# A decoder layer on one core: the rotary table's chain moved next to the opening, and the first tokens loaded from ScalarE's queue

## The chip, the cores and the metric

The kernel runs on one core of a Trainium2 chip. The core has five engines that work side by side and wait for each other through semaphores: TensorE (PE in the profile; PEld is its loading of weights), VectorE (DVE), ScalarE (ACT), GpSimd (POOL) and SyncE (SP). Here SyncE only issues transfers (SPq in the profile). Matrix products go to PSUM, everything else lives in SBUF, and 16 DMA engines bring weights and tokens from HBM.

The metric is device time in microseconds for one execution, as the median of several runs. The profile is taken from one further execution; its span runs from the first to the last instruction of the core.

## The reference: what is computed

One layer of a decoder with 256 positions (batch 1), model width 1024, all in float32:

```python
xn = rmsnorm(h, norm_mix_g)
q_a, k_a, v_a, q_b, f_b, i_b, og_b, g_a, g_b = split_cols(xn @ w_in)   # nine widths of 1024
y_a = moba_attention(q_a, k_a, v_a, positions) @ w_br_attn             # rotary on q_a and k_a
y_b = hgrn2(q_b, f_b, i_b, og_b, lb, hgrn_norm_g) @ w_br_hgrn
h = h + (sigmoid(g_a) * y_a + sigmoid(g_b) * y_b) @ w_out
h = h + memory_cross_attention(rmsnorm(h, norm_x_g), rmsnorm(mem, norm_mem_g), wq_x, wkv_x, wo_x)
gu = rmsnorm(h, norm_ffn_g) @ w_ffn_in
h = h + (silu(gu[:, :2816]) * gu[:, 2816:]) @ w_ffn_out
out = rmsnorm(h, final_norm_g)
```

The rotary embedding turns pairs of features of q_a and k_a by an angle, position times inverse frequency. Its sine and cosine are needed once per layer, as two small tables of 256 positions by 32 frequencies. With 256 positions the attention has a single block, so it is plain causal attention.

## The kernel before, in words

**Weights.** All weight matrices are cut on the host into 97 units of 128 x 2048 floats (1 MB), in the order in which TensorE consumes them (`plan`, `lay`). A unit T covers 512 columns and 512 rows, which TensorE takes in four steps of 128 rows for each of two halves of the tokens. Float32 accuracy is made from three products: each operand is split into a rounded high half and the low half that is left, and high x high, high x low and low x high are added up in PSUM (`mm3`, `mm3t`).

**Preparing a unit** is `prep`: a transfer brings the unit into one of two buffers `raw`; ScalarE rounds it to `hi`; the subtraction `lo = raw - hi` (L185) gives the low half. A unit is handled in two pieces of 1024 columns. Of each piece VectorE subtracts 576 columns and GpSimd 448, except for the units listed in `ALONE` (0 to 7), of which VectorE does all. There are three buffers for `hi` and three for `lo`. `nxt` keeps two units prepared ahead of the one in use, so a unit's raw buffer comes free, and the transfer of the unit two later may start, when its subtraction is done.

**The opening.** Units 0 and 1 (the forget gate's columns, upper half of the rows) are loaded in four pieces of 512 columns each, so that TensorE can start early; unit 1 has a buffer of its own. The tokens, transposed, arrive in five pieces: eight groups of 128 features, cut 1, 1, 2, 2, 2. `part_x` multiplies a group by the norm's gain and splits it into Xh and Xl. All these transfers, the small vector `gv` first, are issued by SyncE one after the other, tokens and weights alternating. After them come units 2 and 3, the constants `cst` (with the identity matrix, a mask, and in its last 32 columns the inverse frequencies), `posi` (the positions), unit 4, the tokens H in rows (1 MB), and the masks `lm`; a transfer waits for the completion of the one eight places before it whose semaphore it takes over. TensorE first runs 18 multiplications of zeros (`warm`), then the gate's product from units 0 and 1, then from 2 and 3.

**The norm's factor.** The products are made with the tokens as they are; the factor 1/rms is applied when a result leaves PSUM. ScalarE squares the two halves of H and adds them up (`junk`, `ssqx`), VectorE makes the mean (L274), GpSimd takes it to the power -0.5 (L276): that is `r_x`. VectorE halves it (`r_half`, L444). Four instructions on ScalarE (`fth`, L391) then take the gate's product out of PSUM with that factor, TensorE turns the result (L369), and ScalarE and VectorE write it to fT.

**The rotary chain.** `rope_tables` runs on GpSimd: it multiplies frequencies by positions, reduces the angle to one turn in several steps of added precision, and folds it, 47 small instructions on 128 x 64 elements, each of which needs the one before. Two sines on ScalarE follow, and eight multiplications by `r_x` on GpSimd give the tables Ct and St. It is a generator: `start(rt)` puts it among the background work, of which `tick` takes a step after every unit. Ct and St are used by `ev_rope`, well after q_b, i_b and v_a.

**The order of work.** TensorE's instructions run in the order in which they are written (`manual_schedule`). For the other engines a scheduler in the tile framework chooses the order, except that a few instructions are pinned with `keep_in_program_order`. In the kernel before, it puts GpSimd's work like this: the positions to float, the first of two angle products, r_x, the rest of the chain (45 instructions), then the twelve products `Tt` of the recurrence (L554), then GpSimd's share of unit 8's subtraction, which is the first that it has. Unit 8 is the first one of i_b; TensorE takes it after the second half of q_b.

Of the kernel before, what the change touches and what calls it, by code (L numbers as in the profile page):

```python
# [18 lines left out]
S, D, NK = 256, 1024, 8  # L19
# [18 lines left out]
C_W = 544  # L38
# [31 lines left out]
def lay(ws):  # L70
    out = np.empty((len(ORDER), 128, 2048), np.float32)
    for i, u in enumerate(ORDER):
        if u[0] == "F":
            w = ws[u[1]][:, u[2]:u[2] + 256]
            out[i].reshape(128, 8, 256)[...] = w.reshape(8, 128, 256).transpose(1, 0, 2)
        elif u[0] == "T":
            w = ws[u[1]][u[3] * 512:(u[3] + 1) * 512, u[2]:u[2] + 512]
            out[i].reshape(128, 4, 512)[...] = w.reshape(4, 128, 512).transpose(1, 0, 2)
# [33 lines left out]
def build(tc, A, out):  # L112
    nc = tc.nc
    V, SC, G, PE, SY = nc.vector, nc.scalar, nc.gpsimd, nc.tensor, nc.sync
    with ExitStack() as ctx:
# [26 lines left out]
        cst = cp.tile([128, C_W], F32, name="cst")  # L142
# [12 lines left out]


        ready = {}
# [2 lines left out]
        def prep(tags=None, raw=None):  # L160
            i = made[0]
            made[0] += 1
            first = i < 2
            if raw is None:
                raw = wr.tile([128, 2048], F32, name="raw", tag="raw")
            if tags is None:
                hi = wh.tile([128, 2048], F32R, name="hi", tag="hi")
                lo = wl.tile([128, 2048], F32R, name="lo", tag="lo")
            else:
                hi = big(tags[0], "hix", (128, 2048), F32R)  # L170
                lo = big(tags[1], "lox", (128, 2048), F32R)
            pieces = 4 if first else 2
            n = 2048 // pieces
            if not first:
                SY.dma_start(raw, A["w"][i])
            for c in range(pieces):
                a = slice(c * n, (c + 1) * n)
                if first:
                    SY.dma_start(raw[:, a], A["w"][i][:, a])
                    yield  # L180
                SC.activation(hi[:, a], raw[:, a], AF.Copy)  # L181
                cut = (c + 1) * n - (0 if i in ALONE else POOL_COLS // pieces)
                for eng, b in ((V, slice(c * n, cut)), (G, slice(cut, (c + 1) * n))):
                    if b.start < b.stop:
                        eng.tensor_tensor(lo[:, b], raw[:, b], hi[:, b].bitcast(F32), op=ALU.subtract)  # L185
            ready[i] = (hi, lo)
# [129 lines left out]
        def part_x(k):  # L316
            g1 = gv[:, V_MIX + k:V_MIX + k + 1]
            SC.activation(Xh[:, k], xraw[:, k], AF.Copy, scale=g1)
            V.scalar_tensor_tensor(Xl[:, k], xraw[:, k], g1, Xh[:, k].bitcast(F32),
                                   op0=ALU.mult, op1=ALU.subtract)  # L320

        def take_x(a, b):
            SY.dma_start(xraw[:, a:b], A["xT"][:, a:b])

        for k in range(4):
            if k in (0, 1, 2):
                take_x(k, (1, 2, 4)[k])
            next(opening[0])
            part_x(k)
        run(opening[0])  # L330
        run(opening[1])
        for k in (4, 6):
            take_x(k, k + 2)
        for k in range(4, 8):
            part_x(k)

        lbt = cp.tile([128, 8], F32, name="lbt")
        oml = cp.tile([128, 8], F32, name="oml")
# [101 lines left out]
        for t in range(2):  # L440
            SC.activation(junk[:, t], H[:, t], AF.Square, accum_out=ssqx[:, t:t + 1])
        r_x = rstd_of(ssqx, "x")
        r_half = cp.tile([128, 2], F32, name="r_half")
        V.tensor_scalar(r_half, r_x, 0.5, None, op0=ALU.mult)  # L444
        ev = ev_f(0)
# [6 lines left out]
            t_part(pss[1][t], w, X, t, 1)  # L452
            ev(t, pss[1][t])
        tick()


        Ct = cp.tile([128, 2, 64], F32, name="Ct")
        St = cp.tile([128, 2, 64], F32, name="St")

        def rope_tables():  # L460
            posf = small("posf", [2])
            G.tensor_copy(posf, posi)
            q = cp.tile([128, 7, 2, 32], F32, name="rt")
            ang, m, mh, ml, r, t, u = (q[:, i] for i in range(7))
            for i in range(2):
                G.tensor_scalar(ang[:, i], cst[:, C_IF:C_IF + 32], posf[:, i:i + 1], None, op0=ALU.mult)

            def rnd(o, src, c):
                G.tensor_scalar(o, src, c, None, op0=ALU.mult)
                G.tensor_scalar(o, o, RND, None, op0=ALU.add)  # L470
                G.tensor_scalar(o, o, RND, None, op0=ALU.subtract)

            def acc(o, a, c, b):
                G.tensor_scalar(u, a, float(c), None, op0=ALU.mult)
                G.tensor_tensor(o, u, b, op=ALU.add)

            rnd(m, ang, 1.0 / (TWO_PI * 1024.0))
            rnd(mh, m, 1.0 / 1024.0)
            G.tensor_scalar(mh, mh, 1024.0, None, op0=ALU.mult)
            G.tensor_tensor(ml, m, mh, op=ALU.subtract)  # L480
            yield 1
            acc(r, mh, -D1, ang)
            acc(r, ml, -D1, r)
            acc(r, mh, -D2, r)
            acc(t, ml, -D2, r)
            acc(t, mh, -D3, t)
            rnd(t, t, 1.0 / TWO_PI)
            yield 1
            for a, c in ((t, C1), (ml, D2), (mh, D3), (t, C2), (ml, D3), (t, C3), (m, D4)):
                acc(r, a, -c, r)  # L490
            lim = 3.1415925
            G.tensor_scalar(t, r, lim, -TWO_PI, op0=ALU.is_gt, op1=ALU.mult)
            G.tensor_scalar(ml, r, -lim, TWO_PI, op0=ALU.is_lt, op1=ALU.mult)
            G.tensor_tensor(r, r, t, op=ALU.add)
            G.tensor_tensor(r, r, ml, op=ALU.add)
            yield 1
            G.tensor_scalar(r, r, lim, -lim, op0=ALU.min, op1=ALU.max)
            G.tensor_scalar(t, r, 0.0, -2.0, op0=ALU.is_gt, op1=ALU.mult)
            G.tensor_scalar(t, t, 1.0, None, op0=ALU.add)
            G.tensor_tensor(t, t, r, op=ALU.mult)  # L500
            G.tensor_scalar(t, t, TWO_PI / 4, None, op0=ALU.add)
            for _ in range(4):
                yield 1
            tc.keep_in_program_order(SC.activation(m, r, AF.Sin))
            tc.keep_in_program_order(SC.activation(mh, t, AF.Sin))
            for i in range(2):
                rs = r_x[:, i:i + 1]
                for c in range(2):
                    G.tensor_scalar(Ct[:, i, c * 32:(c + 1) * 32], mh[:, i], rs, None, op0=ALU.mult)
                G.tensor_scalar(St[:, i, 0:32], m[:, i], rs, -1.0, op0=ALU.mult, op1=ALU.mult)  # L510
                G.tensor_scalar(St[:, i, 32:64], m[:, i], rs, None, op0=ALU.mult)

        rt = rope_tables()

        AT = big("B9", "AT", (128, 24, 128))
        at3 = AT[:, 0:16]
# [648 lines left out]
```

## Time and profile before

| | |
|---|---|
| median of 3 runs | 638.72 us (638.44 to 639.66) |
| the profiled execution's own time | 639.19 us |
| its span | 637.4 us |
| mean granted clock of TensorE | 0.991 |
| bytes moved | 107.5 MB, 169 GB/s over the span |
| TensorE busy | 619.7 us, 97% of the span |

The profiled execution took 0.47 us longer than the median, and 1.8 us longer than its own span. In the lines below a group of instructions is named by line, engine, operation and tiles (`out<-in`); times in a timeline are start and duration in microseconds from the span's start, with the idle time before and what ended it in brackets. A row of waits gives who waited for whom, then total, number and longest. Busy time of TensorE is no measure of its efficiency; what can be read is where it stands idle, at which clock it runs, and how far apart its matmuls start.

### The profile page before, as it was taken

The numbers are of one execution on the slowest core, as the hardware profiler recorded it, in microseconds if no ns is written. First come the engines' busy times: TensorE is split into PE (matmuls) and PEld (weight loads), VectorE is DVE, ScalarE is ACT, GpSimd is POOL, SyncE is SP. The second block draws the span as 40 slices with busy tenths as digits, with TensorE's granted clock in tenths as the row PEclk, the third lists the DMA queues.
The fourth block names the chain that finished last, engine by engine and source line by source line (L and its number), as shares of the span: only waits on it lengthen the run. The fifth ranks groups of instructions, "written<-read, shape, count | busy, mean of one in ns | idle before, by whom it ended". The sixth has DMA issues, their size and how long they took to land.

```text
span 637.4 us, 8670 instructions
## 1 busy us (share of the span) xinstructions
PE 619.7 (97%) x3262; PEld 521.4 (82%) x3262; DVE 380.0 (60%) x649; ACT 326.2 (51%) x513; POOL 367.1 (58%) x289
## 2 busy tenths in 40 slices
PE   7996999999999999999999999999999999999995
PEld 6784888888887777778889999888888888888884
DVE  6462677888857777685646446664444444444433
ACT  6683544433457667673455444554444444444433
POOL 0588555455644564446857767656566555666552
PEclk9998999999999999999999999999999999999998
DMA  8760633443533333535544454462355544455511
GB/s 270 297 240 20 249 147 133 164 171 137 190 132 134 133 132 133 198 135 197 196 159 173 174 192 165 173 250 77 132 193 199 192 176 174 189 194 198 198 66 66
DMA packets 17177, 107.52 MB, mean 169 GB/s; under 512 B 2160, under 2 KB 2544, under 8 KB 4720
## 3 DMA queue, kind: packets, MB, share of 16 engines
q1 hardware_dynamic: 17136, 106.98, 46.6%
q8 instruction: 25, 0.41, 0.3%
q14 instruction: 16, 0.13, 0.1%
HBM read 105.92 MB, written 1.05 MB: 168 GB/s over the span
## 4 chain that ended last, share of the span: by engine, by line
PE 89%; POOL 5%; DMA 3%; issue 1%; SPq 1%; ACT 0%; DVE 0%; POOLq 0%; DVEq 0%; ACTq 0%
PE pst L225 13%; PE pst L226 13%; PE pst L227 13%; PE psi L225 6%; PE psi L227 6%; PE psi L226 6%; PE acc L227 3%; PE acc L226 3%; PE acc L225 3%; PE psf L220 2%; PE psf L221 2%; PE psf L222 2%; PE lp L582 2%; DMA H<-xtok 2%; PE pso L225 1%; PE pso L227 1%
## 5 line engine op out<-in xcount | busy, mean ns | idle before, releaser
L185 POOL TENSOR_TENSOR lo<-raw,hi 128x448 fp32r<-128x448 f32 x174 | 271.0, 1572 | 190.0 <-ACT hi L181 183.3
L181 ACT ACTIVATE hi<-raw 128x1024 fp32r<-128x1024 f32 (+1 forms) x194 | 196.3, 1037 | 199.7 <-PE pst L227 62.7
L185 DVE TENSOR_TENSOR lo<-raw,hi 128x576 fp32r<-128x576 f32 (+2 forms) x194 | 194.1, 1005 | 143.5 <-ACT hi L181 126.7
L226 PE MATMUL pst<-lo,Xh 128*128 128x512 f32 x256 | 100.7, 393 | 6.1 <-POOL lo L185 6.1
L225 PE MATMUL pst<-hi,Xh 128*128 128x512 f32 x256 | 103.8, 405 | 0.0
L227 PE MATMUL pst<-hi,Xl 128*128 128x512 f32 x256 | 100.6, 393 | 0.0
L225 PE MATMUL psi<-hi,h2h 128*128 128x512 f32 x176 | 69.6, 396 | 0.0
L227 PE MATMUL psi<-hi,h2l 128*128 128x512 f32 x176 | 68.7, 390 | 0.0
L226 PE MATMUL psi<-lo,h2h 128*128 128x512 f32 x176 | 68.6, 390 | 0.0
L226 PEld LDWEIGHTS pst<-lo,Xh 128*128 128x128 f32 x256 | 48.7, 190 | 15.7 <-POOL lo L185 6.5
L227 PEld LDWEIGHTS pst<-hi,Xl 128*128 128x128 f32 x256 | 48.5, 189 | 10.3
L225 PEld LDWEIGHTS pst<-hi,Xh 128*128 128x128 f32 x256 | 48.6, 190 | 10.1 <-issue 0.7
L227 PEld LDWEIGHTS psi<-hi,h2l 128*128 128x128 f32 x176 | 33.1, 188 | 7.1
L226 PEld LDWEIGHTS psi<-lo,h2h 128*128 128x128 f32 x176 | 33.1, 188 | 6.5
L225 PEld LDWEIGHTS psi<-hi,h2h 128*128 128x128 f32 x176 | 33.1, 188 | 6.5
L225 PE MATMUL acc<-hi,hid 128*128 128x512 f32 x88 | 34.3, 390 | 0.0
L226 PE MATMUL acc<-lo,hid 128*128 128x512 f32 x88 | 34.3, 389 | 0.0
L227 PE MATMUL acc<-hi,hid 128*128 128x512 f32 x88 | 34.3, 389 | 0.0
L1056 DVE SCALAR_TENSOR_TENSOR fu<-psi,r_h,fg 128x256 f32<-128x256 f32 x22 | 10.6, 483 | 26.1 <-ACT fg L1054 26.1
L1054 ACT ACTIVATE fg<-psi,r_h 128x256 f32<-128x256 f32 x22 | 10.5, 475 | 29.9 <-PE psi L227 29.9
L227 PEld LDWEIGHTS acc<-hi,hid 128*128 128x128 f32 x88 | 16.5, 188 | 3.4
L225 PEld LDWEIGHTS acc<-hi,hid 128*128 128x128 f32 x88 | 16.5, 188 | 3.4
(338 smaller groups left out, 1172.1 us busy)
## 6 DMA issues: line engine op xcount, KB each, us to landing
raw<-w SPq DMA_DIRECT2D x95, 1024.0 KB, 4.8
raw<-w SPq DMA_DIRECT2D x8, 256.0 KB, 5.8
H<-xtok SPq DMA_DIRECT2D x1, 1024.0 KB, 10.2
mraw<-mT SPq DMA_DIRECT2D x1, 1024.0 KB, 7.0
out<-H SPq DMA_DIRECT2D x4, 256.0 KB, 2.2
xraw<-xT SPq DMA_DIRECT2D x3, 256.0 KB, 5.9
gfin<-gfin SPq DMA_DIRECT2D x1, 512.0 KB, 4.9
cst<-cst SPq DMA_DIRECT2D x1, 272.0 KB, 8.9
```

The lines of the kernel that those rows point to most:

```text
L181: SC.activation(hi[:, a], raw[:, a], AF.Copy)
L185: eng.tensor_tensor(lo[:, b], raw[:, b], hi[:, b].bitcast(F32), op=ALU.subtract)
L220: PE.matmul(ps, lh, rh, start=first, stop=False)
L221: PE.matmul(ps, lh, rl, start=False, stop=False)
L222: PE.matmul(ps, ll, rh, start=False, stop=last)
L225: PE.matmul(ps, xh, h, start=first, stop=False)
L226: PE.matmul(ps, xh, l, start=False, stop=False)
L227: PE.matmul(ps, xl, h, start=False, stop=last)
L582: PE.matmul(ps[:, j], KS[:, a0 + j], QQ[:, a0 + j], start=True, stop=True)
L1054: SC.activation(g, ps[:, 0:256], AF.Silu, scale=r)
L1056: V.scalar_tensor_tensor(u, ps[:, 256:512], r, g, op0=ALU.mult, op1=ALU.mult)
```

## The change

Six things are done together.

1. `rope_tables` stands right behind the opening's last token work. Its first half (24 instructions, to the end of its second part) is issued there, its second half (parts three and four) right behind r_x. The sines and the tables Ct and St are issued where they were, by `tick`.
2. From there to the end of q_b's products GpSimd is under `manual_schedule`: its instructions run in the order in which they are written. The first half of the chain so stands ahead of r_x, the second half between r_x and Tt. Ct and St come between the subtractions of unit 9 and unit 10.
3. The inverse frequencies get an array and a tile of their own, `ifq` (128 x 32). It and the positions are issued by SyncE right behind the last token piece, ahead of units 2 and 3; the positions stood behind units 2 and 3 and `cst` before.
4. `gv` and the first three token pieces are issued by ScalarE. Its function table's load, which stood first, comes behind the first two of these transfers. SyncE starts with the four pieces of unit 0.
5. On the host, each of the eight pieces of units 0 and 1, and each of the five token pieces, is laid out as one contiguous block.
6. `ALONE` is 0 to 8: VectorE subtracts all of unit 8 as well.

With the new positions the scheduler also changes some of the others' order: on ScalarE the first `fth` stands ahead of the two `hi` instructions of unit 4 and the other three behind them, where all four stood behind; the two first `hi` pieces of unit 0 stand ahead of the second token group; the exponentials of `lbt` come behind the opening. TensorE's order is the same, instruction for instruction.

```diff
-ALONE = range(8)
+ALONE = range(9)
+TOKENS = ((0, 1), (1, 2), (2, 4), (4, 6), (6, 8))
...
+            if i < 2:
+                out[i].reshape(4, 128, 512)[...] = w.reshape(4, 128, 512)
+            else:
+                out[i].reshape(128, 4, 512)[...] = w.reshape(4, 128, 512).transpose(1, 0, 2)
...
+        def piece(ap, a):
+            flat = ap.rearrange("p c -> (p c)")
+            return flat[128 * a.start:128 * a.stop].rearrange("(p c) -> p c", p=128)
...
+        ifq = cp.tile([128, 32], F32, name="ifq")
...
-        SY.dma_start(gv, A["gv"])
+        SC.dma_start(gv, A["gv"])
...
-        warm_act = cp.tile([128, 1], F32, name="warm_act")
-        SC.activation(warm_act, ones, AF.Exp)
...
-                    SY.dma_start(raw[:, a], A["w"][i][:, a])
+                    SY.dma_start(raw[:, a], piece(A["w"][i], a))
...
-        def take_x(a, b):
-            SY.dma_start(xraw[:, a:b], A["xT"][:, a:b])
-
+        def take_x(eng, a, b):
+            eng.dma_start(xraw[:, a:b].rearrange("p k c -> p (k c)"), piece(A["xT"], slice(256 * a, 256 * b)))
+
+        take_x(SC, *TOKENS[0])
+        warm_act = cp.tile([128, 1], F32, name="warm_act")
+        SC.activation(warm_act, ones, AF.Exp)
+        for piece_x in TOKENS[1:3]:
+            take_x(SC, *piece_x)
         for k in range(4):
-            if k in (0, 1, 2):
-                take_x(k, (1, 2, 4)[k])
             next(opening[0])
             part_x(k)
         run(opening[0])
         run(opening[1])
-        for k in (4, 6):
-            take_x(k, k + 2)
+        for piece_x in TOKENS[3:]:
+            take_x(SY, *piece_x)
+        SY.dma_start(ifq, A["ifq"])
+        SY.dma_start(posi, A["pos"])
         for k in range(4, 8):
             part_x(k)
...
+        rt = rope_tables()
+        region = tc.manual_schedule(engines={mybir.EngineType.Pool})
+        region.__enter__()
+        next(rt)
+        next(rt)
...
         SY.dma_start(cst, A["cst"])
-        SY.dma_start(posi, A["pos"])
...
         r_x = rstd_of(ssqx, "x")
+        next(rt)
+        next(rt)
...
         start(rt)
         for c in range(2):
             gemm_t(X, ev_q(c))
+        region.__exit__(None, None, None)
```

More of the change, by code (lines that the diff above doesn't have):

```diff
@@ L77, in lay @@
             w = ws[u[1]][u[3] * 512:(u[3] + 1) * 512, u[2]:u[2] + 512]
-            out[i].reshape(128, 4, 512)[...] = w.reshape(4, 128, 512).transpose(1, 0, 2)
+            if i < 2:
+                out[i].reshape(4, 128, 512)[...] = w.reshape(4, 128, 512)
+            else:
+                out[i].reshape(128, 4, 512)[...] = w.reshape(4, 128, 512).transpose(1, 0, 2)
         elif u[0] == "I":
@@ L137, in small @@
             return sp.tile([128] + list(shape), F32, name=name)
+        def piece(ap, a):
+            flat = ap.rearrange("p c -> (p c)")
+            return flat[128 * a.start:128 * a.stop].rearrange("(p c) -> p c", p=128)
         def bank(name, shape=(128, 512)):
             return sm.tile(list(shape), F32, name=name, tag="sm")
-        cst = cp.tile([128, C_W], F32, name="cst")
+        cst = cp.tile([128, C_IF], F32, name="cst")
         gv = cp.tile([128, 56], F32, name="gv")
@@ L331, in build, with rope_tables, rnd, acc @@
         run(opening[1])
-        for k in (4, 6):
-            take_x(k, k + 2)
+        for piece_x in TOKENS[3:]:
+            take_x(SY, *piece_x)
+        SY.dma_start(ifq, A["ifq"])
+        SY.dma_start(posi, A["pos"])
         for k in range(4, 8):
             part_x(k)
+        Ct = cp.tile([128, 2, 64], F32, name="Ct")
+        St = cp.tile([128, 2, 64], F32, name="St")
+        def rope_tables():
+            posf = small("posf", [2])
+            G.tensor_copy(posf, posi)
+            q = cp.tile([128, 7, 2, 32], F32, name="rt")
+            ang, m, mh, ml, r, t, u = (q[:, i] for i in range(7))
+            for i in range(2):
+                G.tensor_scalar(ang[:, i], ifq, posf[:, i:i + 1], None, op0=ALU.mult)
+            def rnd(o, src, c):
+                G.tensor_scalar(o, src, c, None, op0=ALU.mult)
+                G.tensor_scalar(o, o, RND, None, op0=ALU.add)
+                G.tensor_scalar(o, o, RND, None, op0=ALU.subtract)
+            def acc(o, a, c, b):
+                G.tensor_scalar(u, a, float(c), None, op0=ALU.mult)
+                G.tensor_tensor(o, u, b, op=ALU.add)
+            rnd(m, ang, 1.0 / (TWO_PI * 1024.0))
+            rnd(mh, m, 1.0 / 1024.0)
+            G.tensor_scalar(mh, mh, 1024.0, None, op0=ALU.mult)
+            G.tensor_tensor(ml, m, mh, op=ALU.subtract)
+            yield 1
+            acc(r, mh, -D1, ang)
+            acc(r, ml, -D1, r)
+            acc(r, mh, -D2, r)
+            acc(t, ml, -D2, r)
+            acc(t, mh, -D3, t)
+            rnd(t, t, 1.0 / TWO_PI)
+            yield 1
+            for a, c in ((t, C1), (ml, D2), (mh, D3), (t, C2), (ml, D3), (t, C3), (m, D4)):
+                acc(r, a, -c, r)
+            lim = 3.1415925
+            G.tensor_scalar(t, r, lim, -TWO_PI, op0=ALU.is_gt, op1=ALU.mult)
+            G.tensor_scalar(ml, r, -lim, TWO_PI, op0=ALU.is_lt, op1=ALU.mult)
+            G.tensor_tensor(r, r, t, op=ALU.add)
+            G.tensor_tensor(r, r, ml, op=ALU.add)
+            yield 1
+            G.tensor_scalar(r, r, lim, -lim, op0=ALU.min, op1=ALU.max)
+            G.tensor_scalar(t, r, 0.0, -2.0, op0=ALU.is_gt, op1=ALU.mult)
+            G.tensor_scalar(t, t, 1.0, None, op0=ALU.add)
+            G.tensor_tensor(t, t, r, op=ALU.mult)
+            G.tensor_scalar(t, t, TWO_PI / 4, None, op0=ALU.add)
+            for _ in range(4):
+                yield 1
+            tc.keep_in_program_order(SC.activation(m, r, AF.Sin))
+            tc.keep_in_program_order(SC.activation(mh, t, AF.Sin))
+            for i in range(2):
+                rs = r_x[:, i:i + 1]
+                for c in range(2):
+                    G.tensor_scalar(Ct[:, i, c * 32:(c + 1) * 32], mh[:, i], rs, None, op0=ALU.mult)
+                G.tensor_scalar(St[:, i, 0:32], m[:, i], rs, -1.0, op0=ALU.mult, op1=ALU.mult)
+                G.tensor_scalar(St[:, i, 32:64], m[:, i], rs, None, op0=ALU.mult)
@@ L454, in build @@
         tick()
[L457 to L511, printed above, removed]
@@ L1137, in feats, with by_piece @@
         return np.ascontiguousarray(v[0].T.reshape(8, 128, S).transpose(1, 0, 2))
+    def by_piece(v):
+        return np.concatenate([v[:, i:j].reshape(-1) for i, j in TOKENS]).reshape(128, 8 * S)
     ws = {k: a[k][0] for k in ("w_in", "w_br_attn", "w_br_hgrn", "w_out", "wq_x", "wkv_x", "wo_x",
@@ L1144 @@
         "w": lay(ws),
-        "xT": feats(a["x"]),
+        "xT": by_piece(feats(a["x"])),
         "xtok": tokens(a["x"]),
         "mT": feats(a["mem"]),
+        "ifq": np.ascontiguousarray(cst[:, C_IF:]),
         "pos": np.ascontiguousarray(a["positions"][0].reshape(2, 128).T),
@@ L1152 @@
         "gfin": np.ascontiguousarray(a["final_norm_g"].reshape(1, D)),
-        "cst": cst,
+        "cst": np.ascontiguousarray(cst[:, :C_IF]),
         "lm": lm,
```

1 line of the change is left out of this document (removed).

## The prediction

> **What bounds the kernel now.** I read the page's first part, then who TensorE (PE) waits for, then the chain of waits, then windows round the one long wait, then the engines' timelines of the opening.
>
> ```profile
> PE 619.7 (97%) x3262; PEld 521.4 (82%) x3262; DVE 380.0 (60%) x649; ACT 326.2 (51%) x513; POOL 367.1 (58%) x289
> ```
> ```profile
> PE pst L226 <- POOL lo L185: 6.1, 1, 6.1
> PE psg L429 <- ACT hi L181: 2.0, 2, 1.2
> ...
> PE psg L226 <- DVE lo L185: 0.7, 1, 0.7
> ```
>
> PE is busy 97% and, once started, waits for another engine only in these places: 2.7 us in the opening, and once 6.1 us for the low half of a weight unit that GpSimd (POOL) makes. Everything after that wait runs at PE's own pace, so whatever PE gains or loses up to there should reach the end one for one. The chain of waits tells why POOL was late:
>
> ```profile
> 23.23 2.20 ACT junk L441 x4
> ...
> 25.71 0.73 POOL r_x L276
> 26.44 0.37 POOL rt L466
> ...
> 54.43 0.37 POOL rt L501
> 54.80 1.01 POOL Tt L554
> ...
> 61.07 1.14 POOL lo L185
> 62.25 0.80 PE pst L226
> 63.05 0.43 PE pst L227
> ...
> 619.88 0.23 PE acc L227
> ```
>
> From 26.44 to 54.80 POOL works off the rotary chain, then the products Tt, and only at 61.07 the weight unit. The windows (busy time and instructions of PE, PEld, DVE, ACT, POOL, then granted clock, DMA share, GB/s) show a second price of that wait:
>
> ```profile
> 55.00:56.20 1.20, 1.16 (x6) 0.62 (x4) 0.00 (x0) 0.69 (x1) 1.12 (x2) 1.00 0.02 7
> 56.20:59.20 3.00, 0.00 (x0) 0.00 (x0) 0.00 (x0) 0.00 (x0) 2.61 (x7) 1.00 0.00 0
> 59.20:62.20 3.00, 0.00 (x0) 0.00 (x0) 0.00 (x0) 0.00 (x0) 2.69 (x7) 0.51 0.00 0
> 62.20:66.20 4.00, 3.95 (x10) 3.15 (x11) 0.00 (x0) 0.00 (x0) 3.29 (x3) 0.51 0.42 125
> 66.20:70.00 3.80, 3.80 (x23) 3.29 (x22) 0.65 (x1) 1.74 (x2) 0.60 (x1) 1.00 1.00 407
> ```
>
> About 3 us into the idle time the clock falls to half, and it stays there until about 66.1. About nine matmuls run in that stretch at 0.43 us instead of 0.23: 9 x 0.20 = 1.8 us. The wait is worth 6.1 + 1.8 = 7.9 us.
>
> **The change part by part.** The sum is made against the profiled execution's own 639.19 us (span 637.4); the median of the three runs is 638.72, so I subtract from the median.
>
> *The rotary chain moves forward: -7.9.* Its second half now stands right behind r_x and its first half ahead of it. The rows I price it with:
>
> ```profile
> 20.86 0.18 POOL L462 CAST posf<-posi 128x2 f32<-128x2 int32 x1 [20.44 <-DMA posi<-pos]
> 21.15 2.51 POOL L466 TENSOR_SCALAR rt<-cst,posf 128x32 f32<-128x32 f32 x1
> 27.35 0.38 POOL L470 TENSOR_SCALAR rt<-rt 128x64 f32<-128x64 f32 x1
> 28.27 1.41 POOL L469 TENSOR_SCALAR rt<-rt 128x64 f32<-128x64 f32 x1
> 29.76 1.09 POOL L470 TENSOR_SCALAR rt<-rt 128x64 f32<-128x64 f32 x1
> 31.85 0.33 POOL L480 TENSOR_TENSOR rt<-rt 128x64 f32<-128x64 f32 x1
> 35.33 0.32 POOL L475 TENSOR_TENSOR rt<-rt 128x64 f32<-128x64 f32 x1
> 40.89 0.37 POOL L471 TENSOR_SCALAR rt<-rt 128x64 f32<-128x64 f32 x1
> ```
> ```profile
> 14.37 1.81 DVE L319 SCALAR_TENSOR_TENSOR Xl<-xraw,gv,Xh 128x256 fp32r<-128x256 f32 x4 [0.43 <-ACT Xh L318]
> 21.14 2.36 DVE L185 TENSOR_TENSOR lo<-raw,hi 128x1024 fp32r<-128x1024 f32 x2 [0.23 <-ACT hi L181]
> 26.48 0.17 DVE L444 TENSOR_SCALAR r_half<-r_x 128x2 f32<-128x2 f32 x1 [0.85 <-POOL r_x L276]
> 28.22 2.40 DVE L185 TENSOR_TENSOR lo<-raw,hi 128x1024 fp32r<-128x1024 f32 x2 [1.57 <-ACT hi L181]
> 34.94 0.53 DVE L384 TENSOR_SCALAR fT<-fT__353,gate_a,gate_b 128x256 f32<-128x256 f32 x1
> ```
>
> A quiet POOL step takes 0.37 us (scalar form) or 0.33 (two tensors), each with 0.08 to the next. Beside a VectorE subtraction lo<-raw,hi it takes 1.41, 1.09 or 2.51 instead; beside fT, which reads PSUM, it keeps 0.32. From 26.44 to 41.26 (end of the step at 40.89) run 16 scalar and 6 two-tensor steps: 14.8 us, of which 16 x 0.45 + 6 x 0.40 = 9.6 are work and 5.2 are stretch from six subtractions of 1.2 us, 0.87 each.
>
> After the change, 24 steps stand ahead of r_x: 0.3 + 17 x 0.45 + 6 x 0.40 = 10.3 us quiet. r_x itself, the second half (23 steps, about 10 us and three pairs of subtractions, 15 us), the twelve Tt (6.3 us, 54.80 to 61.07) then end near 51, and PE wants that weight unit at 56 or later. Besides, unit 8 is now split by VectorE alone (one more in ALONE), and POOL's next one, unit 9, is wanted a unit later still. So the 6.1 us go, and the half clock with them. VectorE's extra share (1024 columns of a piece at 1.2 us instead of 576, so 2 x 1.2 x 448/1024) is 1.0 us and due by PE's 56; in the stretch in which its queue comes to it VectorE is busy less than half the time,
>
> ```profile
> 45.00:50.00 5.00, 5.00 (x28) 4.25 (x27) 2.11 (x3) 3.17 (x4) 4.23 (x10) 1.00 0.56 213
> ```
>
> so nothing; if that cover went, it would cost the 1.0 us. The eight Ct/St steps move ahead of unit 10; that unit is wanted two units (over 11 us) after the Sin that releases them: nothing.
>
> *The price: r_x now waits for the first half.* It starts when positions land. They are moved from behind two whole weight units and cst to right behind the last token piece:
>
> ```profile
> 13.82 1.84 ACT L318 ACTIVATE Xh<-xraw,gv 128x256 fp32r<-128x256 f32 x4 [0.61 <-DMA xraw<-xT]
> 17.45 2.01 ACT L181 ACTIVATE hi<-raw 128x1024 fp32r<-128x1024 f32 x2 [1.79 <-DMA raw<-w]
> 29.04 2.50 ACT L391 ACTIVATE fth<-psg,r_half 128x512 f32<-128x512 f32 x4
> ```
>
> The last token piece was there by the third Xh, 14.7. With the gain of the opening (0.7, below) positions land near 14.0. Then 10.3 quiet, plus the subtractions of units 2 and 3 (four, 0.87 each: 3.5), plus the four Xl of 0.45, never seen beside POOL: between nothing (like fT) and 4 x 0.45 x 0.73 = 1.3 (like lo); they too read two SBUF tensors, but some are over by then, so 0.7. Sum 28.5 for the start of r_x, against 25.71; the sum of squares will be ready before 25.45. Bounds 26.5 and 30.5.
>
> Who is queued behind it: r_half and then unit 4's subtraction on VectorE; on ScalarE, where the order now puts one fth ahead of unit 4's two hi and three behind them, all of these. From r_x's start: 0.73, then 0.2 for r_half, fth 0.65, two hi 2.0, second fth 0.65: 4.3 us. PE's transposes need both:
>
> ```profile
> 30.66 0.60 PE L369 MATMUL fT__353<-cst,fth 128*128 128x128 f32 x4
> ```
>
> They started at 30.66 with PE busy up to them; now 28.5 + 4.3 = 32.8. PE is 2.1 us behind there, after an idle time of 2.1 + 0.7 = 2.8 us. That delay is kept to the end: +2.1 (bounds 0.1 and 4.1, from 26.5 and 30.5).
>
> *Tokens on ScalarE's queue, contiguous first pieces: 0.7 earlier in the opening, then used up.*
>
> ```profile
> 1.16 0.42 SPq L323 DMA_DIRECT2D xraw<-xT  x1
> 1.63 0.42 SPq L179 DMA_DIRECT2D raw<-w  x1
> ```
> ```profile
> 1.50:5.40 3.90, 3.78 (x18) 3.57 (x18) 1.85 (x11) 1.42 (x4) 0.00 (x0) 1.00 0.69 170
> 8.50:18.80 10.30, 10.24 (x45) 8.29 (x45) 7.42 (x14) 7.70 (x15) 0.00 (x0) 1.00 1.02 384
> ```
>
> The first weight piece is issued at 0.7 instead of 1.63. From 8.5 on the transfers are the limit (share 1.02, 384 GB/s), so all that counts is what moves before: 170 GB/s for 3.9 us, where 384 would save 2.2 us. Whether address order helps there the trace cannot tell; bounds -0.5 (two queues in each other's way) and 1.9. I take 0.7, nearer to the 0.9 of the earlier issue. ScalarE pays four issues of 0.42 with its table load between them, before it has data; SyncE's queue loses these four and gains the one for ifq (16 KB): nothing for both, as long as the transfers are the limit. The opening's 0.7 is worth something at the end only if r_x isn't late; here PE just waits 0.7 longer at the transposes.
>
> Sum: 638.72 - 7.9 + 2.1 = **632.9 us**.
>
> [...] In the rows a subtraction of 1.2 us holds POOL 0.87 us. [...] The clock fell 3 us into the idle time above, and mine is 2.8. [...]
>
> **The rivals.**
> - *The first half is done in time* (0.18). Positions land at 12.5, or VectorE's work falls before or after. The earliest r_x is the sum of squares, about 25; then 25 + 4.3 is before 30.66 - 0.7 and PE keeps the opening's gain too: 638.72 - 7.9 - 0.7 = 630.1, down to 629.4. Against it: 10.3 quiet us from 14.0 already end at 24.3, and units 2 and 3 are split inside that time.
> - *POOL is held longer and PE's clock falls* (0.16). The row at 21.15 is stretched by 2.14 us beside 2.36 of subtraction, 0.91 of it. On 4.7 + 1.8 us that gives 5.9 and r_x at 30.2; PE is 3.8 late and idle for 4.5, more than the 3 us of the windows, so another 1.8 goes: 638.72 - 7.9 + 5.6 = 636.4.
> - *A new wait replaces the old one* (0.08), at unit 9 or 10: POOL still does Tt, Ct/St and two units there. A third of the old wait back: 635.
> - *Slower* (0.08): r_x so late that it eats the gain. From 7.9 - 1.8 = 6.1 us late on PE, an r_x at 30.66 + 6.1 - 4.3 = 32.5, it decides. That needs positions at 18 instead of 14, as if they still queued behind a weight unit (they landed at 20.86 before): at 19.5, r_x at 34.0 gives 7.6 + 1.8 - 7.9, 640.2.
> - *Nothing* (0.05): 638.7, if gain and price cancel.
>
> **How the numbers follow.** The forecast's own case has 0.45, with 631 to 635 for r_x between 26.6 and 30.6; the others as given, which adds to 1. A measurement of this kernel can tell about 0.2% (1.3 us) from no change. Faster by more: 0.45 + 0.18 + 0.16 + 0.08 = 0.87, same 0.05, slower 0.08. The range leaves out the last two cases: from 629.4 to 636.8.
>
> **What would show it.** Right: no wait of PE for POOL's lo near 56 and full clock there; positions landing near 14 and POOL's chain starting with them; r_x near 28.5, behind POOL's own step and not behind the sum of squares; a new wait of PE of 2 to 3 us at the transposes fT, for ScalarE's fth; Tt over by about 51. Wrong: r_x still at 25 to 26 (then more is gained), a half clock near 33, or a wait at units 8 to 10 in the old one's place.

## The result, and the profile after

The changed kernel takes 632.63 us (median of 5 executions, 631.75 to 634.07). On the same chip the kernel before took 638.44 us (638.3 to 639.66). The ratio is 0.9899, with a 95% interval of 0.9887 to 0.9912: 6.4 us less. The profiled execution of the changed kernel is the longest of its five: 634.07 us, span 632.3.

The page's first part for the changed kernel, then its table of who TensorE waits for (total us, times, longest):

```profile
PE 620.0 (98%) x3262; PEld 521.5 (82%) x3262; DVE 384.8 (61%) x649; ACT 325.1 (51%) x513; POOL 366.7 (58%) x287
```
```profile
PE fT__408 L445 <- ACT fth L467: 2.3, 2, 2.1
...
PE psg L504 <- ACT hi L189: 0.7, 1, 0.7
PE psg L504 <- ACT Xh L326: 0.3, 1, 0.3
```

TensorE has the same work, 620 us in 3262 instructions. The wait of 6.1 us for GpSimd's lo is gone. In its place stands a new one of 2.3 us at the transposes fT, for ScalarE's fth.

How far the gain has come, and whether any of it is given back, is read at one late landmark in the two chains of waits: TensorE's transposes h1T, and the last piece of the end. Kernel before, then changed kernel (start, us, what):

```profile
345.05 0.87 PE h1T L904 x8
...
630.88 1.79 issue
```
```profile
340.00 0.87 PE h1T L923 x8
...
625.82 1.79 issue
```

From h1T to the end both take 285.8 us. The changed kernel is 5.05 us ahead at h1T and 5.06 at the end, so in these two executions all of the difference arises before, and nothing of it is lost later.

The first stage, engine by engine (start, us, engine, line, operation; in brackets how long the engine had been idle, which is no point in time, and what ended it). GpSimd of the changed kernel:

```profile
12.94 0.96 POOL L356 CAST posf<-posi 128x2 f32<-128x2 int32 x1 [12.52 <-DMA posi<-pos]
14.01 1.60 POOL L360 TENSOR_SCALAR rt<-ifq,posf 128x32 f32<-128x32 f32 x2
...
17.52 1.16 POOL L364 TENSOR_SCALAR rt<-rt 128x64 f32<-128x64 f32 x1
18.76 1.09 POOL L365 TENSOR_SCALAR rt<-rt 128x64 f32<-128x64 f32 x1
19.93 1.32 POOL L373 TENSOR_SCALAR rt<-rt 128x64 f32<-128x64 f32 x1
21.33 1.04 POOL L374 TENSOR_TENSOR rt<-rt 128x64 f32<-128x64 f32 x1
...
27.99 0.73 POOL L284 TENSOR_TENSOR r_x<-v__339,nhalf 128x2 f32<-128x2 f32 x1
...
44.68 1.03 POOL L572 TENSOR_TENSOR Tt<-fT 128x512 f32<-128x512 f32 x1
...
53.57 1.16 POOL L193 TENSOR_TENSOR lo<-raw,hi 128x448 fp32r<-128x448 f32 x1
```

VectorE, ScalarE and TensorE of the changed kernel in the same stretch:

```profile
11.37 2.49 DVE L193 TENSOR_TENSOR lo<-raw,hi 128x512 fp32r<-128x512 f32 x4
13.78 1.66 DVE L327 SCALAR_TENSOR_TENSOR Xl<-xraw,gv,Xh 128x256 fp32r<-128x256 f32 x4
...
17.22 2.40 DVE L193 TENSOR_TENSOR lo<-raw,hi 128x1024 fp32r<-128x1024 f32 x2 [0.61 <-ACT hi L189]
19.79 2.40 DVE L193 TENSOR_TENSOR lo<-raw,hi 128x1024 fp32r<-128x1024 f32 x2 [0.18 <-ACT hi L189]
24.04 0.17 DVE L282 TENSOR_SCALAR v__339<-ssqx 128x2 f32<-128x2 f32 x1 [1.85 <-ACT junk L516]
28.75 0.17 DVE L521 TENSOR_SCALAR r_half<-r_x 128x2 f32<-128x2 f32 x1 [4.54 <-POOL r_x L284]
```
```profile
29.02 0.69 ACT L467 ACTIVATE fth<-psg,r_half 128x512 f32<-128x512 f32 x1 [5.01 <-DVE r_half L521]
29.60 1.99 ACT L189 ACTIVATE hi<-raw 128x1024 fp32r<-128x1024 f32 x2
31.50 1.83 ACT L467 ACTIVATE fth<-psg,r_half 128x512 f32<-128x512 f32 x3
```
```profile
29.19 0.39 PE L235 MATMUL psg<-hi,Xl 128*128 128x512 f32 x1
29.76 0.33 PE L445 MATMUL fT__408<-cst,fth 128*128 128x128 f32 x1 [0.18 <-ACT fth L467]
32.23 0.55 PE L445 MATMUL fT__408<-cst,fth 128*128 128x128 f32 x3 [2.14 <-ACT fth L467]
```

What to see: GpSimd's first step starts at 12.94, when the positions are there. The sum of squares' scaled value v stands at 24.04 + 0.17 = 24.2, but r_x starts at 27.99, right behind GpSimd's own chain. ScalarE is idle for 5.01 us until r_half, and then does one fth, the two hi of unit 4 and only then the second fth. TensorE is through with its matmuls at 29.6 and gets the second fth at 32.2.

Windows of the changed kernel (TensorE, its weight loads, VectorE, ScalarE, GpSimd: busy us and instructions; then granted clock, DMA share, GB/s):

```profile
30.00:32.00 2.00, 0.09 (x1) 0.00 (x0) 1.32 (x2) 2.00 (x3) 1.75 (x4) 1.00 0.00 0
32.00:33.70 1.70, 1.47 (x10) 1.39 (x11) 1.17 (x1) 1.70 (x5) 1.53 (x3) 0.99 0.00 0
33.70:37.10 3.40, 3.40 (x9) 2.66 (x8) 2.88 (x3) 2.95 (x5) 2.97 (x6) 0.50 0.71 272
...
55.00:60.00 5.00, 5.00 (x24) 4.14 (x23) 1.71 (x3) 3.09 (x7) 2.19 (x3) 1.00 0.52 185
```

At 55 to 60, where the 6.1 us stood, TensorE is busy throughout at full clock. But from 33.7 to 37.1, after it has been working again for 1.5 us, its clock is half: at 0.43 us a matmul instead of 0.23 these 3.4 us cost about 1.6.

### The profile page after: what moved, and what is told of

It is laid out like the page before. It is cut to its first block, busy times and chain, and to the rows that moved or that the text cites. A ratio compares the mean times of both kernels' runs of the same rounds, so it can differ in the third digit from the quotient of the medians.

```text
span 632.3 us, 8666 instructions
## 1 busy us (share of the span) xinstructions
PE 620.0 (98%) x3262; PEld 521.5 (82%) x3262; DVE 384.8 (61%) x649; ACT 325.1 (51%) x513; POOL 366.7 (58%) x287
## 4 chain that ended last, share of the span: by engine, by line
PE 94%; issue 3%; POOL 2%; ACT 1%; DVE 0%; POOLq 0%; ACTq 0%
PE pst L233 14%; PE pst L235 14%; PE pst L234 14%; PE psi L233 6%; PE psi L235 6%; PE psi L234 6%; PE acc L235 3%; PE acc L234 3%; PE acc L233 3%; PE psf L229 2%; PE psf L228 2%; PE psf L230 2%; PE lp L600 2%; PE pso L233 1%; PE pso L235 1%
## 5 line engine op out<-in xcount | busy, mean ns | idle before, releaser
L193 DVE TENSOR_TENSOR lo<-raw,hi 128x576 fp32r<-128x576 f32 (+2 forms) x194 | 198.1, 1028 | 126.5 <-ACT hi L189 125.3
L233 PE MATMUL psi<-hi,h2h 128*128 128x512 f32 x176 | 69.6, 395 | 0.0
L235 PEld LDWEIGHTS acc<-hi,hid 128*128 128x128 f32 x88 | 16.5, 188 | 3.4
L234 PEld LDWEIGHTS acc<-lo,hid 128*128 128x128 f32 x88 | 16.5, 188 | 3.4
```

The costliest lines, as they stand in the source:

```text
L233: PE.matmul(ps, xh, h, start=first, stop=False)
L234: PE.matmul(ps, xh, l, start=False, stop=False)
L235: PE.matmul(ps, xl, h, start=False, stop=last)
```

## The experiments

None of the eleven kernels leaves out any of the reference's work. The gain in the last column is (1 - ratio) times 638.7 us, so that the runs of different chips stand on one scale; "wait" is TensorE's longest one behind the opening.

| kernel | median us (range) | ratio to before [95%] | wait | gain us |
|---|---|---|---|---|
| the change | 632.63 (631.75-634.07) | 0.9899 [0.9887, 0.9912] | fth 2.3 | 6.4 |
| before + unit 8 alone | 637.08 (636.51-637.31) | 0.9966 [0.9953, 0.9978] | QQ 3.9 | 2.2 |
| change without unit 8 alone | 633.05 (631.38-634.5) | 0.9902 [0.9885, 0.992] | fth 2.1 | 6.3 |
| change with the old opening | 633.82 (633.07-635.31) | 0.992 [0.9906, 0.9935] | fth 1.8 | 5.1 |
| before + the opening | 637.32 (636.23-638.73) | 0.9969 [0.996, 0.9979] | lo 5.6 | 2.0 |
| before + opening + unit 8 | 634.92 (633.65-635.76) | 0.9933 [0.9919, 0.9947] | QQ 3.6 | 4.3 |
| change, r_x earlier | 630.24 (629.08-631.26) | 0.9863 [0.9846, 0.988] | QQ 0.4 | 8.8 |
| change, hi ahead of fth | 630.24 (630.02-631.19) | 0.9869 [0.9852, 0.9885] | fth 0.6 | 8.4 |
| both of these | 629.43 (628.85-630.67) | 0.9854 [0.9838, 0.9869] | none | 9.3 |
| change, filler in the wait | 633.26 (632.3-633.85) | 0.991 [0.9895, 0.9924] | fth 1.2 | 5.7 |
| change, r_x later | 642.01 (641.01-642.79) | 1.0042 [1.0029, 1.0056] | fth 9.8 | -2.7 |

### Unit 8 split by VectorE alone, in the kernel before

```diff
-ALONE = range(8)
+ALONE = range(9)
```

> The kernel before with one edit: unit 8 is subtracted by VectorE alone; chain, r_x and transfers stay. Theory A (what counts is which unit first needs GpSimd after the chain): before, the chain and Tt end at 61.07; unit 9's first piece would then be ready at 62.2, and TensorE, not held at 56, would ask for it at about 63.5, so the 6.1 us and the half clock (7.9 together) go without the chain being moved: 630.6. Rival B (the chain has to move): the wait passes on to unit 9 with 3 us or more, the clock falls again: 634 to 637.

Measured 637.08 us: theory A is wrong, and rival B's picture is the right one (its time is missed by 0.1 us). TensorE's longest wait behind the opening, and the chain of waits of this kernel from 62 on:

```profile
PE l L536 <- ACT QQ L403: 3.9, 1, 3.9
```
```profile
62.36 2.22 POOL lo L185 x2
64.60 4.97 DMA raw<-w
69.68 2.00 ACT hi L181 x2
71.68 0.49 ACT QQ L403
```

The wait does not vanish, it moves one unit on. GpSimd is as late as before, so unit 9's lo comes at 62.4. That frees a raw buffer late, the next weight unit lands late (69.6), and its hi stands on ScalarE's queue ahead of QQ, which TensorE needs. The clock falls again too: in this chain TensorE's matmuls take 0.43 us each from 74.50 to 76.21, and 0.23 from 76.55 on. Taking one unit off GpSimd is worth 2.2 of the 7.9 us; whether taking off more units would do without moving the chain was not tried.

### The change without it

```diff
-ALONE = range(9)
+ALONE = range(8)
```

> The changed kernel with unit 8 shared between VectorE and GpSimd again. Theory A: the moved chain lets GpSimd off at 53.6, unit 8's two pieces take 2.3 us, TensorE asks for them at about 59: no wait, 632.6 as with the change (within 0.7). Rival D (the moved chain alone isn't enough, unit 8 has to leave GpSimd): TensorE waits at unit 8 again, over 634.

Measured 633.05 us, 0.9902 against 0.9899: no difference. There is no wait at unit 8 either; the only one behind the opening is `fth`, 2.1 us. With the chain moved, this edit is worth nothing.

### The opening undone, and the opening alone

In the first kernel the tokens, gv and the first weight pieces come as before, by SyncE's queue and strided; the rest is the change. The second is the kernel before with these transfers changed and nothing else.

```diff
-        SC.dma_start(gv, A["gv"])
+        SY.dma_start(gv, A["gv"])
...
-                    SY.dma_start(raw[:, a], piece(A["w"][i], a))
+                    SY.dma_start(raw[:, a], A["w"][i][:, a])
...
-        for piece_x in TOKENS[1:3]:
-            take_x(SC, *piece_x)
+            if k in (0, 1, 2):
+                take_x(k, (1, 2, 4)[k])
```

> The changed kernel with gv and tokens on SyncE's queue again and strided pieces; chain, ifq, positions and unit 8 as in the change. Theory A: the positions land with the last token piece, 1 to 1.8 us later than 12.94, r_x and TensorE's transposes follow by the same: 633.5 to 634.5. Rival C (the transfers carry much of the gain): over 635.5. Rival E (they do nothing): 632.6.

> The kernel before with only the transfers changed: gv and three token pieces on ScalarE's queue, contiguous pieces. Theory A: the sum of squares and so the chain behind r_x come 1.2 to 1.4 us earlier, TensorE's opening by about 1.1; the wait for GpSimd at unit 8 stays about as long: 637.1 to 637.4. Rival C: 634 or less. Rival E: 638.4.

Measured 633.82 and 637.32 us: the opening is worth 1.3 us in the change and 2.0 us alone. GpSimd's first step and r_x of the kernel with the old opening:

```profile
14.53 0.46 POOL L347 CAST posf<-posi 128x2 f32<-128x2 int32 x1 [14.11 <-DMA posi<-pos]
...
28.68 0.73 POOL L278 TENSOR_TENSOR r_x<-v__339,nhalf 128x2 f32<-128x2 f32 x1
```

In the change, the opening's transfers bring GpSimd's first step 1.6 us earlier (12.94 instead of 14.53) and r_x 0.7 us, and with r_x the transposes (32.23 instead of 32.92). So about half of the 1.3 us can be followed in the traces by way of r_x, although TensorE waits longer at the transposes (2.3 against 1.8 us) for having arrived there earlier. The other half stands only in the medians, whose intervals overlap (one goes up to 0.9912, the other starts at 0.9906). In the kernel before, the forecast met the time but not the way: r_x comes 0.5 us earlier (25.18 instead of 25.71), not 1.2 to 1.4, in a profiled execution that is slower than its median (638.07 us). The windows of the changed kernel's opening, against 170 GB/s and a DMA share of 0.69 before:

```profile
1.50:5.40 3.90, 3.84 (x18) 3.84 (x18) 0.41 (x4) 1.50 (x3) 0.00 (x0) 1.00 0.96 276
```

Whether the queue or the order of addresses does it was not taken apart.

### Opening and unit 8, without the chain

This is the kernel before with both edits, so all of the change but the rotary chain and the earlier transfers of its inputs (ifq and the positions).

> The kernel before with everything of the change but the rotary chain: the opening's transfers and unit 8 split by VectorE alone. Theory A (by the two runs of each alone, 637.3 and 637.1, which add up, since one lies in the opening and one at units 8 and 9; the chain behind r_x keeps GpSimd late for unit 9, and TensorE then waits for it in QQ's place): 635.2 to 636.2, with a wait of TensorE of 3 to 5 us for QQ or for unit 9's raw, none for lo of unit 8, and r_x near 25.2. Rival B (chain move worth nothing by itself): 632 to 633.5, no wait over 2 us.

Measured 634.92 us, 0.3 below the forecast's lower end (r_x, too, is earlier than forecast, 23.6 instead of 25.2): 4.3 us gained, where the two alone gave 2.0 + 2.2. They add up, since one lies in the opening and the other at units 8 and 9. The wait for QQ stays:

```profile
PE l L545 <- ACT QQ L412: 3.6, 1, 3.6
```

The chain's move, as it was made and with what it costs at r_x, is worth 6.4 - 4.3 = 2.1 us on top of that.

### r_x earlier

One part of the chain less ahead of r_x: 11 steps ahead, 36 behind.

```diff
         region.__enter__()
         next(rt)
-        next(rt)
...
         r_x = rstd_of(ssqx, "x")
+        next(rt)
         next(rt)
         next(rt)
```

> The changed kernel with one part fewer of the rotary chain ahead of r_x: 11 steps stand ahead, 36 behind, nothing else differs. Theory A (the 2.3 us of TensorE's wait at the transposes are the price of 13 chain steps ahead of r_x, and the half clock behind it comes from that wait): r_x starts at the sum of squares, 24.2 to 24.6 instead of 28.0; no wait of TensorE at the transposes, no half clock near 34; the chain ends some 2 us later than 44.7 and the Tt near 55, still ahead of unit 9's use; 632.6 - 2.3 - up to 1.6 = 629.0 to 630.5. Rival B (r_x is not what holds the transposes; ScalarE's two hi are): wait of 1.5 us or more stays, 631.5 to 633. Rival C (what moves behind r_x makes GpSimd late for unit 9): a wait of TensorE for lo or for a unit near 62 appears, 631 or more.

Measured 630.24 us: theory A. r_x follows the sum of squares at once, the wait at the transposes is gone, and the clock stays at 1.00 in all windows from 28 to 70. Its waits in the profiled execution and r_x:

```profile
PE psg L503 <- ACT Xh L326: 1.7, 1, 1.7
...
PE l L554 <- ACT QQ L478: 0.4, 1, 0.4
```
```profile
25.60 0.73 POOL L284 TENSOR_TENSOR r_x<-v__326,nhalf 128x2 f32<-128x2 f32 x1 [3.05 <-DVE v__326 L282]
```

r_x stands at 25.60, not 24.3, only because this execution's opening was 1.4 us slower (1.7 us of waiting for Xh against 0.3). What moved behind r_x makes a wait of 0.4 us near 70: that is the beginning of rival C, at a small price.

### hi ahead of the first fth

r_x stays late; unit 4 is prepared behind the squares, and the first fth is kept behind its two hi on ScalarE's queue.

```diff
-        run(prep())
         SY.dma_start(H, A["xtok"])
-        SY.dma_start(lm, A["lm"])
...
-        w = by_k(nxt(), 4)
+        w = by_k(nxt(1), 4)
...
+        run(prep())
+        SY.dma_start(lm, A["lm"])
+        pin.append(1)
         ev = ev_f(0)
...
-                SC.activation(th[t], ps, AF.Tanh, scale=r_half[:, t:t + 1])
+                act = SC.activation(th[t], ps, AF.Tanh, scale=r_half[:, t:t + 1])
+                if pin:
+                    tc.keep_in_program_order(act)
+                    pin.clear()
```

> The changed kernel with only ScalarE's order round the first tanh changed: unit 4's two hi (2.0 us) stand ahead of the first fth instead of between the first and the second. r_x stays where it is. Theory A (two things make the price: r_x at 28.0, and 2.0 us of hi that stand between the two fth while ScalarE idles 5 us before them): the two fth follow each other from about 29.0, transposes start at 30.4 to 30.7, the wait is 0.7 to 1.1 instead of 2.3, no half clock; 630.0 to 631.3. Rival B (unit 4's raw is not there early, or r_x alone sets the place): the wait stays above 1.8, 632 to 633.

Measured 630.24 us: theory A, and as much as the earlier r_x. ScalarE and TensorE's wait:

```profile
25.14 2.01 ACT L189 ACTIVATE hi<-raw 128x1024 fp32r<-128x1024 f32 x2 [1.37 <-DMA raw<-w]
28.48 2.42 ACT L469 ACTIVATE fth<-psg,r_half 128x512 f32<-128x512 f32 x4 [1.33 <-DVE r_half L524]
```
```profile
PE fT__408 L445 <- ACT fth L469: 0.6, 2, 0.3
```

The two hi fit into the 5 us in which ScalarE had nothing else. So the price had two halves, and to remove either removes nearly all of it: an r_x some 4 us late, and 2.0 us of hi between the two fth that TensorE waits for.

> Both of the last but one: 11 chain steps ahead of r_x, and unit 4's hi ahead of the first fth. Theory A: with r_x early there is no wait left at the transposes, so the order of ScalarE adds nothing: within 0.6 us of the kernel with 11 steps ahead, 629.0 to 630.5. Rival B (hi ahead of fth delays the first fth when r_x is early, since the raw of unit 4 lands later than r_x): a wait of 0.5 to 2 us at the transposes comes back, 630.5 to 632.

With both, 629.43 us. TensorE has no wait behind the opening, and the half clock is gone. The gain over one of them alone is 0.5 to 1.0 us by the ratios, less than their intervals can tell apart. It is the fastest of the kernels here, 1.5% below the kernel before.

### A filler in the wait, for the clock

Seven more matmuls of 128x512, whose result nothing reads, right ahead of the transposes.

```diff
+        fill = bank("fill")
+        for _ in range(7):
+            PE.matmul(fill, Xh[:, 0, :128], Xh[:, 0:2].rearrange("p k c -> p (k c)"), start=True, stop=True)
         tick()
```

> The changed kernel with seven more matmuls of 128x512 into a bank that nothing reads, right ahead of the transposes: about 1.6 us of work inside TensorE's wait of 2.3. The wait's end does not move. Theory A (the half clock from 33.7 to 37.1 comes from the window that holds this wait, and costs about 1.6 us in the executions that have it): no half clock in the profile, clock 0.998 or more in all runs, 631.0 to 632.0 and a smaller spread than 631.8 to 634.1. Rival B (the half clock has another origin, or costs nothing at the end): half clock still there, 632.3 to 633.5.

Measured 633.26 us: the time lies in rival B's range, while the half clock is gone, as theory A has it. So the clock follows the wait, but this run does not show its price at the end. TensorE with the late landmark h1T, the windows and the new wait of this kernel, and last the same landmark in the timeline of the changed kernel:

```profile
29.25 1.75 PE L533 MATMUL fill<-Xh 128*128 128x512 f32 x7
...
32.32 0.55 PE L445 MATMUL fT__416<-cst,fth 128*128 128x128 f32 x3 [1.20 <-ACT fth L467]
...
338.31 1.04 PE L926 MATMUL h1T<-cst,H 128*128 128x128 f32 x8
```
```profile
30.00:34.00 4.00, 2.80 (x17) 2.19 (x16) 2.48 (x2) 4.00 (x6) 3.49 (x7) 1.00 0.00 0
34.00:40.00 6.00, 6.00 (x32) 5.02 (x32) 3.88 (x5) 4.84 (x8) 5.34 (x9) 1.00 0.85 279
```
```profile
PE xT L1003 <- DVE xp L997: 0.6, 1, 0.6
```
```profile
339.84 1.03 PE L923 MATMUL h1T<-cst,H 128*128 128x128 f32 x8
```

The transposes come when they came before (32.32 against 32.23), the half clock is gone in the profile, and the clock over the whole run is 0.997 or 0.998 in all four executions. At h1T the kernel is 339.84 - 338.31 = 1.5 us ahead of the changed kernel, as theory A has it. By the end of the profiled execution 0.4 us of it is left (span 631.9 against 632.3): 0.6 us go in a wait near 408 that the changed kernel does not have, 0.5 were not found, and the median is no better than that of the changed kernel. The planner gave ScalarE, VectorE and GpSimd another order here, behind the filler, so this kernel differs in more than the clock.

A second way to the price of the half clock are the executions themselves. The changed kernel and its twin without unit 8's edit take the same time within their intervals. Of their ten executions three had a mean clock of 0.998: 631.38, 631.75 and 632.04, mean 631.7. Six had 0.993 or 0.994, less than any execution of the kernels without a long wait (0.996 to 0.998): 632.6 to 634.5, mean 633.4. That is 1.7 us, about what the windows gave (1.6); it is 1.4 when each is taken against the kernel before on its own chip (638.44 and 639.25). It is a comparison and no experiment, and the mean clock is a rough sign: the kernel with unit 8 alone has 0.996 in its profiled execution, with a half clock in it.

### r_x later

One part more of the chain ahead of r_x: 42 steps ahead, 5 behind.

```diff
         region.__enter__()
         next(rt)
         next(rt)
+        next(rt)
...
         r_x = rstd_of(ssqx, "x")
         next(rt)
-        next(rt)
```

> The changed kernel with one part more of the rotary chain ahead of r_x: 42 steps ahead, 5 behind. Theory A (r_x behind chain steps is paid one for one at the transposes, and the half clock comes behind an idle time long enough): 18 steps, 14 scalar at 0.45 and 4 of two tensors, more ahead, so some 7.9 us, with no subtraction beside them since unit 4's hi waits behind the first fth; r_x at 35.5 to 36.2, TensorE's wait at the transposes near 10 us, half clock inside or behind it for certain; 632.6 + 7.9 + up to 1.6 = 640 to 642, slower than the kernel before. Rival B (the delay is caught up later, in waits that come after the transposes): 634 to 638.

Measured 642.01 us, slower than the kernel before. TensorE's wait and r_x:

```profile
PE fT__408 L446 <- ACT fth L468: 9.8, 2, 7.8
```
```profile
35.02 0.73 POOL L284 TENSOR_TENSOR r_x<-v__357,nhalf 128x2 f32<-128x2 f32 x1
```

r_x is 35.02 - 27.99 = 7.0 us later, TensorE's wait 7.5 us longer, the time by the ratios 9.1 us longer. The transposes come at 39.31 instead of 32.23, and the spans of the two profiled executions (639.2 and 632.3), which both have a half clock, differ by 6.9. So r_x's delay is paid in full, as theory A has it, and nothing behind it is caught up. The 9.1 compares medians, and not every execution of the changed kernel has the clock of a half-clock stretch; what makes up its rest of some 2 us was not taken apart.

## Why the prediction was right, and where it was not

The forecast of 632.9 us met the median within 0.3 us, and the mechanism it named is there: the old wait is gone, and a late r_x takes part of the gain back at the transposes. That the number is so close is partly luck. The five executions lie at 631.75 and 632.04 (clock 0.998), 632.63 (0.996), and 632.98 and 634.07 (0.993 and 0.994), with the median between the two groups, and errors of opposite sign cancel in it. Its steps:

- **The 7.9 us of the old wait: right.** No wait and full clock at 55 to 60. The prediction gave this to the chain's move, and counted unit 8's edit as help. The runs confirm that: the edit alone only passes the wait on to unit 9 and QQ (2.2 us), and beside the moved chain it is worth nothing. Where the price at the transposes is removed as well, the gain is 8.4 to 9.3 us, room enough for the 7.9 and a part of the opening's.
- **Positions land near 14.0: they landed at 12.9,** 1.1 us earlier. With the old opening they land at 14.5, so the opening brought 1.6 us instead of the 0.7 that I took; without it I would have been 0.2 too late (14.7).
- **14.5 us from there to r_x: it took 15.05** (12.94 to 27.99). The four large subtractions cost, each on the step that met it, 1.16 - 0.37, 1.09 - 0.38, 1.32 - 0.37 and 1.04 - 0.32: 3.2 us against 3.5. Beside Xl two steps took 1.60 together, instead of 0.82 at a quiet 0.37 and a gap of 0.08: 0.8 against 0.7. What I had left out: the first step runs beside the last of the opening's small subtractions (11.37 to 13.86) and takes 0.96 instead of 0.18, another 0.8. The step that starts at 17.52 inside a subtraction ends at 18.68, 0.23 us behind the end of the first of the two, at 18.45. Of the 1.23 us of this first subtraction, 0.30 were over before the held step started, and behind it only 0.23 of the 0.37 that a quiet step takes were left. The rival with a falling clock took 0.91 of the whole time of the subtractions (4.7 us, twice the row of 2.36) and of the four Xl (1.8, the row of 1.81); that is too high here: of 4.8 us of large subtractions (2 x 2.40) 3.2 were lost, of 1.66 us of Xl 0.8.
- **r_x at 28.5, the transposes behind the second fth at 32.8, a wait of 2.8: measured 27.99, 32.23 and 2.3.** From r_x to the transposes 4.24 us, as reckoned (4.3). Where r_x was moved both ways, TensorE's wait followed it.
- **An idle time of 2.8 us, counted without a loss of clock: wrong.** This is the step that failed. It was an estimate from the one fall in the kernel before, 3 us into its idle time; no run shows that so much is needed. The clock fell in the profiled execution after an idle time of 2.14 us, and in its twin's after the same; by their mean clocks in some six of ten executions. The price is 1.6 us by the windows and 1.4 to 1.7 by the executions. Other shifts hid it: the transposes came 0.6 us earlier than forecast, which against the median covers part of it. In the profiled execution the sum is -7.9 + 1.6 (transposes at 32.23 for 30.66) + 1.6 = -4.7; measured 634.07 - 639.19 = -5.1. Of the rival with a falling clock (636.4) the clock came true, without the later r_x and without the 3 us of idle time that it asked for.
- **The opening's 0.7, "then used up": too small, and only in part used up.** TensorE starts its last matmul ahead of the transposes 1.2 us earlier (29.19 for 30.43), and by the medians the opening is worth 1.3 us in the change, 2.0 alone, just past the upper bound of 1.9 that I had from the GB/s.
- **Tt over by about 51: over at 53.6.** The twelve products took 44.68 to 53.57, 8.9 us instead of 6.3; VectorE has subtractions beside them now (45.21 to 46.79 and 48.73 to 52.35), and had nothing to do from 56.2 to 62.2 before. That was still ahead of TensorE's need: there was no wait at units 8 to 10, which settles that rival.

The rival in which the first half is done in time (630.1 us) is what the kernel with an earlier r_x makes true: 630.24. The slower rival, with its deciding point at an r_x of 32.5, is what the kernel with a later one makes true: r_x at 35.0, 642.01. What the prediction did not see is the cheaper remedy: ScalarE's five idle us ahead of the first fth, into which the two hi that it counted as price fit.

## What to carry to other kernels

When a long chain is moved off one wait, look at which small, early result it now stands ahead of on the same engine; here one part of the chain less ahead of r_x was worth 2.4 us, as much as the move itself had brought on top of the other edits (2.1 us). Taking one unit off a late engine passed most of the wait on here (2.2 of 7.9 us gained), through the buffer that it frees late, to what is queued behind the next transfer. And a price of "late result + work queued behind it" can be cut at either end: an idle time on the engine that holds the queue is a place to move that work into.

## What the runs showed of the hardware that I had not expected

- The half clock came after less than 3 us of idle time. In the changed kernel 2.14 us of idle time, followed by 1.5 us of work, was followed by half clock for 3.4 us, and its twin without unit 8's edit shows the same. With 1.8 us idle (the old opening), 1.2 (the filler) or 0.6 (hi ahead of fth) the profile shows none. The twin, behind its idle time (which ends at 31.25):

```profile
31.90:35.40 3.50, 3.50 (x13) 2.71 (x11) 2.45 (x4) 3.50 (x6) 2.99 (x7) 0.54 0.53 194
```

  The half clock of the changed kernel lasted from 33.7 to 37.1, and by the mean clocks the same program has it in some executions (0.993, 0.994) and not in others (0.998). The 3.4 us ahead of the drop, 30.3 to 33.7, held 1.47 us of work. Half of that are transposes, of which no run here shows whether they hold the clock up; without them, 3.4 us pass between the last matmul ahead of them (29.19 + 0.39) and the next behind them (32.96).
- The opening is not steady. The sums of the windows over the first 20 us, of the changed kernel and of the one with the earlier r_x, whose opening has the same transfers, in one execution each:

```profile
sum 20.00, PE 17.34 PEld 14.03 DVE 13.09 ACT 12.59 POOL 6.55; mean PE 4.33 PEld 3.51 DVE 3.27 ACT 3.15 POOL 1.64
```
```profile
sum 20.00, PE 15.99 PEld 12.80 DVE 12.16 ACT 11.29 POOL 5.66; mean PE 4.00 PEld 3.20 DVE 3.04 ACT 2.82 POOL 1.42
```

  TensorE is busy for 17.3 us in the one and 16.0 in the other: these two executions differ there by 1.3 us, as much as the opening's edit is worth in the change.
